# Gating products of reloaded activations placed behind the previous step's split, and 84 instead of 72 up products ahead

## The chip, the cores and the metric

The kernel runs on one core of one Trainium2 chip. The metric is the device time of one execution in microseconds (us); of several runs the median counts, and lower is better.

## The reference

Two blocks run one after the other on 256 latent and 256 context tokens of width 1024, in float32. The change lies in the first layer of the first block, in its feed-forward part over 16,384 experts:

```python
scores = einsum('bthpd,hpkd->bthpk', qr, subkeys)      # two halves of a query, 128 keys each
s1, i1 = top_k(scores[..., 0, :], 16); s2, i2 = top_k(scores[..., 1, :], 16)
top, pos = top_k(s1[..., :, None] + s2[..., None, :], 16)
eidx = (i1 * 128 + i2)[pos]; gate = softmax(top)
act = gelu(einsum('ted,td->te', u[eidx], h))
out = einsum('te,ted->td', gate * act, v[eidx])
```

Each token selects 8 x 16 experts; each expert is a row of `u` and a row of `v`.

## The kernel before

**Dense experts.** For three of the four token tiles (384 tokens) the kernel computes all 16,384 experts densely. They are cut into 128 chunks of 128. An *up* (`up0`, L1133) is one chunk's product with the 384 token columns: 24 matmuls of 384 columns in PSUM tile `pu`, a GELU on ScalarE into `act`, 128 x 384. Float32 is kept by splitting each operand into a high and a low half and multiplying three times (`mm3`, L292): a weight tile is loaded into `wr` (4 buffers), ScalarE casts the high half (`wh`, L286), VectorE subtracts it to get the low half (`wl`, L287). The loader `S0` has three `wh`/`wl` pairs, for ups and downs alike.

A *down* (`Down`, L849) multiplies the gated activations of one chunk with 128 rows of `v`: 18 matmuls of 512 columns, for three token tiles, accumulated in six PSUM banks over all 128 chunks. So no down can be finished before all gates are known.

**Gates.** `route0` (L1144) computes the queries and keys, the selection (`select`, VectorE), and then writes the gates of all 384 tokens as a dense table (`scatter`, L807, into `gd0` in DRAM), by one-hot matmuls of 128 columns. It is a generator: at each `yield x, y` the loop at L1205 adds `x` to a credit and traces that many ups beside the routing, and `y` to the steps of `own` (below). Ups that are computed before the gates exist are written to DRAM (`actd`, L1140) and read back later.

**The main loop** (L1250) runs over `j` = 0 to 129:

```python
again(j + 5)                       # reload of act j+5, ten act buffers
if j + 2 >= NA and done[0] < 128:
    up0()
if j < 128:
    weigh0(j)
...
if j >= LAG:                       # LAG = 2
    down0(j - LAG)
own_steps(0.5 if j + 2 < NA else 1.4)
```

`weigh0(i)` (L1226) loads the gates of eight chunks at once (`gsc`, 1.5 MB, two buffers), multiplies `act` by the gate on VectorE (L1232, called *the product* below), casts the high half `Wh` on ScalarE (L1236) and subtracts for the low half `Wl` on VectorE (L1237); `Wh` and `Wl` have four buffers. With `NA` = 72 the loop has two parts: a *reload part*, with downs alone, whose activations come back from DRAM, and a *late part*, in which each step has an up and a down.

**The fourth tile.** `own` (L1099) treats 128 tokens by gathering each one's experts: for each of 128 slots an indirect DMA from GpSimd's queue brings 8 KB per token (`uv`, 1 MB, four buffers), VectorE computes the dot product with `u` (L1118) and adds the weighted `v` (L1113). `own_steps(x)` places such steps behind the instruction in `mark[0]`, the last `Wl` of the loop (or the last one-hot in the scatter).

**What sets the order.** The engines' order is made by a scheduler at build time, by priorities and a model of durations; `tc.issue_after(ins)` adds an edge that keeps what is traced inside the block behind `ins` on its own engine. Each engine, and each DMA queue, then runs its list in order, and an instruction that waits holds up all that stands behind it. Loads and reloads are issued by SyncE (SP).

Of the kernel before, what the change touches and what calls it, by code (L numbers as in the profile page):

```python
# [29 lines left out]
OP = mybir.AluOpType  # L30
# [15 lines left out]
PK = 4  # L46
FA = 4
AH1 = 22
NA = 72
LAM_INIT = 0.8 - 0.6 * math.exp(0.0)  # L50


# [168 lines left out]
def body(ctx: ExitStack, tc: tile.TileContext, ap, stop=99):  # L221
    nc = tc.nc

    def pool(es, name, bufs=1, space=None, side=None):
        if space is None:
            return es.enter_context(tc.tile_pool(name=name, bufs=bufs, side=side, reuse_waits="tile"))
        return es.enter_context(tc.tile_pool(name=name, bufs=bufs, space=space))
# [35 lines left out]
    def pw(shape=(128, 512), name="pw"):  # L263
        return psP.tile(list(shape), F32, name=name, tag="ps")
# [32 lines left out]
    def prod_b(src, h, t0, n, sx=None, alloc=None, eng=None):  # L297
        wh, wl = (sx or S0).load(src, (128, DK, 128), eng=eng)
        ps = (alloc or pu)()[:, :n]
        c0 = t0 - h.base  # L300
        for k in range(DK):
            mm3(ps, wh[:, k], wl[:, k], h.hi[:, k, c0:c0 + n], h.lo[:, k, c0:c0 + n], k == 0, k == DK - 1)
        return ps
# [20 lines left out]
    def new_h(p, tag="h", base=0, n=512):  # L324
        h = K()
        h.base = base
        h.hi = p.tile([128, DK, n], F32R, name=tag + "hi")
        h.lo = p.tile([128, DK, n], F32R, name=tag + "lo")
        return h
# [29 lines left out]
    def sums(name):  # L359
        return sm.tile([128, 2], F32, name=name, tag=name, bufs=4)  # L360

    def sq_half(src, ss, nt):
        junk = sm.tile([128, 512], BF16, name="junk", tag="junk", bufs=1)
        nc.scalar.activation(junk, src, AF.Square, accum_out=ss[:, nt:nt + 1])
# [104 lines left out]
    def drain(it):  # L469
        for _ in it:  # L470
            pass

    def add_gated(t, nt, ps, g):
        ns = slice(nt * 512, nt * 512 + 512)
        tmp = sm.tile([128, 512], F32, name="agt", tag="agt", bufs=1)
        nc.vector.tensor_tensor(tmp, ps, g[:, ns], op=OP.mult)
        r = res(t)
        nc.vector.tensor_tensor(r[:, ns], r[:, ns], tmp, op=OP.add)
# [229 lines left out]
    def top16(rp, s, v, i, n):  # L708
        w = rp.tile([128, n], F32, name="mr", tag=f"mr{n}", bufs=2)
        nc.vector.max(v[:, 0:8], s)  # L710
        nc.vector.max_index(i[:, 0:8], v[:, 0:8], s)
        nc.vector.match_replace(w, v[:, 0:8], s, -3.0e38)
        nc.vector.max(v[:, 8:16], w)
        nc.vector.max_index(i[:, 8:16], v[:, 8:16], w)
# [88 lines left out]
    def turned(rp, T, tag="TT", tiles=range(2)):  # L803
        TT = rp.tile([128, 2, 4, 128], F32, name="TT", tag=tag, bufs=1)
        for t in tiles:
            ps = pw((128, 3, 128))
            for a in range(3):  # L807
                nc.tensor.transpose(ps[:, a], T[:, a, t], ident)
            nc.scalar.copy(TT[:, t, :3], ps)
            nc.vector.tensor_scalar(TT[:, t, 3], TT[:, t, 1], -1.0, None, op0=OP.mult)  # L810
        return TT

    mark = [None]
# [280 lines left out]
    gd0 = dp.tile([24, 128, 128, 16], F32, name="gd0")  # L1094
    actd = dp.tile([NA, 128, 384], F32, name="actd")
    eid = tp0.tile([128, 128], U32, name="eid")
# [31 lines left out]
    def act0():  # L1128
        return tp0.tile([128, 24, 16], F32, name="act", tag="act", bufs=10)
# [3 lines left out]
    def up0():  # L1133
        i = done[0]
        done[0] += 1
        pg = prod_b(ap["ut0"][i], hh, 0, 384)
        a = act0()
        nc.scalar.activation(a, pg.rearrange("p (a b) -> p a b", b=16), AF.Gelu)
        if i < NA:
            nc.scalar.dma_start(actd[i], a.rearrange("p a b -> p (a b)"))  # L1140
        else:
            late[i] = a

    def route0():  # L1144
        et, es = ExitStack(), ExitStack()
        hp = pool(et, "turned0")
        kp = pool(es, "keys0")
        rp = pool(es, "route0")
        tvs = [kp.tile([128, 2, 2, 8, 16], F32, name=f"tv{p}") for p in range(2)]
        tis = [kp.tile([128, 2, 2, 8, 16], U32, name=f"ti{p}") for p in range(2)]  # L1150
        Ts = [kp.tile([128, 3, 2, 128], F32, name=f"T{p}") for p in range(2)]

        def sel(p, half):
            return select(rp, tvs[p], tis[p], half, Ts[p], 2, (eid, egt) if p else None)
        s0 = sel(1, 0)
        for c in range(16):
            pq = prod_b(ap["wq0"][c], hh, 0, 512, eng=nc.gpsimd if c >= 4 else None)
            qT = kp.tile([128, 512], F32, name="qT", tag="qT", bufs=2)
            nc.scalar.copy(qT, pq)
            skey = kp.tile([128, 128], F32, name="skey", tag="skey", bufs=2)  # L1160
            nc.sync.dma_start(skey, ap["skey0"][:, c])
            ps = pw((128, 4, 128))
            for a in range(4):
                nc.tensor.matmul(ps[:, a], qT[:, a * 128:(a + 1) * 128], skey, start=True, stop=True)
            with tc.high_priority(offset=HP):
                for a in range(4):
                    p, t = divmod(a, 2)
                    top16(kp, ps[:, a], tvs[p][:, c // 8, t, c % 8], tis[p][:, c // 8, t, c % 8], 128)
            if c >= 8:
                next(s0, None)  # L1170
            yield (0.2 if c < 8 else 0.7), 0
        for _ in s0:
            yield 0.6, 0
        for _ in sel(1, 1):
            yield 0.6, 0
        for half in range(2):
            for _ in sel(0, half):
                yield 0.6, 0
        TX = turned(hp, Ts[1], "TTx", (0,))
        TC = turned(hp, Ts[0], "TTc")  # L1180
        es.close()
        yield 0, None
        op = pool(et, "scatter0")
        for k, TT in ((2, TX[:, 0]), (0, TC[:, 0]), (1, TC[:, 1])):
            for _ in scatter(op, TT, gd0[8 * k:8 * k + 8], 2):
                yield 0.42, 0.2
        et.close()

    def mods_ahead():
# [5 lines left out]
    def own_steps(x):  # L1195
        due[0] += x
        while due[0] >= 1:
            with tc.issue_after(mark[0].ins):
                next(mine, None)
            due[0] -= 1  # L1200
# [3 lines left out]
    for x, y in route0():  # L1204
# [7 lines left out]
        credit += x  # L1212
        while credit >= 1 and done[0] < NA:
            up0()
            credit -= 1
        own_steps(y)
    drain(fill)
    while done[0] < NA:
        up0()
# [4 lines left out]
    gates, acts, later = [None], {}, []  # L1224

    def weigh0(i):  # L1226
        if i % 8 == 0:
            gates[0] = gp0.tile([128, 24, 8, 16], F32, name="gsc", tag="gsc", bufs=2)
            nc.sync.dma_start(gates[0].rearrange("p a b c -> p a (b c)"),
                              gd0[:, :, i:i + 8].rearrange("a p i t -> p a (i t)"))  # L1230
        a = acts.pop(i) if i < NA else late.pop(i)
        nc.vector.tensor_tensor(a, a, gates[0][:, :, i % 8], op=OP.mult)  # L1232
        wh = ep.tile([128, 384], F32R, name="Wh", tag="Wh", bufs=4)
        wl = ep.tile([128, 384], F32R, name="Wl", tag="Wl", bufs=4)
        af = a.rearrange("p a b -> p (a b)")
        nc.scalar.copy(wh, af)  # L1236
        mark[0] = nc.vector.tensor_tensor(wl, af, wh, op=OP.subtract)  # L1237
        later.append((wh, wl))

    def again(i):  # L1240
        if i < NA:
            acts[i] = act0()
            nc.sync.dma_start(acts[i].rearrange("p a b -> p (a b)"), actd[i])
# [6 lines left out]
    for j in range(128 + LAG):  # L1250
        again(j + 5)
# [4 lines that stand above are left out]
        if j == 128 + LAG - 4:  # L1256
            drain(mine)
            for nt in range(2):
                add_gated(3, nt, yown[:, nt * 512:(nt + 1) * 512], g2x)
            css[3] = sums("nss")  # L1260
            for nt in range(2):
                sq_half(resx[:, 1, nt * 512:(nt + 1) * 512], css[3], nt)
            eO.close()
            h1 = new_h(pool(eM, "mixh1", 1, side="right"))
            c1 = ms[0, 1].coefs(1, 0, 1)
        if j >= LAG:
            down0(j - LAG)
        own_steps(0.5 if j + 2 < NA else 1.4)
    for t in (2, 3, 0, 1):
        with tc.high_priority(offset=2 * HP):  # L1270
            if t != 3:
# [433 lines left out]
```

## Time and profile before

| | us |
|---|---|
| median of three runs (lowest, highest) | 3767.36 (3761.19, 3768.62) |
| the profiled execution's own time | 3762.31 |
| its span | 3760.5 |
| TensorE busy in the span | 3518.7 (94%) |
| VectorE busy | 2509.4 (67%) |
| ScalarE busy | 1726.1 (46%) |
| GpSimd busy | 582.5 (15%) |

The span is what the profiler saw from the first to the last instruction; the own time is 1.8 us longer. A busy share is an average over stages with different limits, so the stages of the first layer's experts are told apart by time: keys and selection to about 735 us, scatter to 976 us, the turn to the main loop to 1004 us, the reload part to 1380 us, the late part to 1850 us. Granted clock 1.00 means that TensorE had its full 2.4 GHz all through a stretch.

### The profile page before, as it was taken

The page shows a single profiled execution, that of the slowest core. Times are in us where ns is not written, and L with a number is a line of the kernel's source. Part 1 is how long each engine was busy: PE and PEld are TensorE (multiplying, and loading weights), DVE is VectorE, ACT ScalarE, POOL GpSimd, SP SyncE. Part 2 cuts the span into 40 slices and gives each one's busy share as a digit, 9 for nine tenths or more (in the row PEclk, how much of TensorE's full clock was granted, in tenths as well). Part 3 has the DMA queues.
Part 4 walks back from the last instruction along what each step waited for, and adds up shares of the span by engine and source line. Part 5 has one row for each costly group of instructions (what it writes and reads, how often), then busy time and mean ns, then how long its engine had stood idle before and what let it go on. Part 6 is the DMA issues. An engine that isn't in the chain of part 4 may idle for free. (4 is left out here: it accounts for less than half of the span.)

```text
span 3760.5 us, 57378 instructions
## 1 busy us (share of the span) xinstructions
PE 3518.7 (94%) x21201; PEld 3044.2 (81%) x21201; DVE 2509.4 (67%) x5109; ACT 1726.1 (46%) x3173; POOL 582.5 (15%) x618
## 2 busy tenths in 40 slices
PE   7998998999887799999998899999999989898899
PEld 5776777799766679999886889988998868798798
DVE  5456698488655578787666799655555556656854
ACT  4323323466422234444443558444444445655464
POOL 0000110276200012222000327000000012001200
PEclk9999999999998999999999999999999989999999
DMA  6325447787977788888455456766665565654373
GB/s 232 125 97 183 143 160 278 286 286 276 308 262 247 250 285 322 321 325 323 162 163 181 165 171 242 249 209 214 216 212 197 188 216 185 207 180 150 125 261 105
DMA packets 293073, 818.89 MB, mean 218 GB/s; under 512 B 25303, under 2 KB 133496, under 8 KB 271096
## 3 DMA queue, kind: packets, MB, share of 16 engines
q1 hardware_dynamic: 263992, 666.83, 52.6%
q0 software_dynamic: 18432, 134.23, 9.7%
q10 hardware_dynamic: 10368, 14.16, 1.0%
q8 instruction: 168, 2.75, 0.3%
q14 instruction: 113, 0.93, 0.1%
HBM read 755.29 MB, written 59.83 MB: 217 GB/s over the span
## 5 line engine op out<-in xcount | busy, mean ns | idle before, releaser
L287 DVE TENSOR_TENSOR wl<-wr,wh 128x1024 fp32r<-128x1024 f32 x812 | 999.0, 1233 | 578.5 <-ACT wh L286 575.9
L286 ACT CAST wh<-wr 128x1024 fp32r<-128x1024 f32 x840 | 877.6, 1047 | 830.1 <-PE pu L294 497.2
L293 PE MATMUL pu<-hxhi,wh 128*128 128x256 f32 x1984 | 561.5, 283 | 6.3 <-ACT wh L286 4.1
L295 PE MATMUL pu<-hxhi,wl 128*128 128x256 f32 x1984 | 560.8, 283 | 0.8 <-DVE wl L287 0.8
L294 PE MATMUL pu<-hxlo,wh 128*128 128x256 f32 x1984 | 559.5, 282 | 0.2 <-DVE hxlo L404 0.2
L293 PE MATMUL pacc<-wh,Wh 128*128 128x512 f32 x1280 | 508.8, 398 | 0.0
L294 PE MATMUL pacc<-wl,Wh 128*128 128x512 f32 x1280 | 508.5, 397 | 0.0
L295 PE MATMUL pacc<-wh,Wl 128*128 128x512 f32 x1280 | 506.5, 396 | 0.0
L293 PE MATMUL pu<-hhhi,wh 128*128 128x384 f32 (+1 forms) x1152 | 403.3, 350 | 6.0 <-ACT wh L286 4.7
L295 PE MATMUL pu<-hhhi,wl 128*128 128x384 f32 (+1 forms) x1152 | 399.8, 347 | 6.7 <-DVE wl L287 6.4
L294 PE MATMUL pu<-hhlo,wh 128*128 128x384 f32 (+1 forms) x1152 | 398.6, 346 | 0.0
L293 PEld LDWEIGHTS pu<-hxhi,wh 128*128 128x128 f32 x1984 | 373.9, 189 | 15.2 <-ACT wh L286 4.9
L294 PEld LDWEIGHTS pu<-hxlo,wh 128*128 128x128 f32 x1984 | 374.2, 189 | 7.8 <-DVE hxlo L404 0.7
L295 PEld LDWEIGHTS pu<-hxhi,wl 128*128 128x128 f32 x1984 | 375.0, 189 | 1.2 <-DVE wl L287 1.0
L295 PEld LDWEIGHTS pacc<-wh,Wl 128*128 128x128 f32 x1280 | 242.9, 190 | 58.1
L1105 POOL DMA_INDIRECT uv<-in_uv_dram,eid x128 | 158.7, 1240 | 830.5 <-DVE yown L1113 682.5
L293 PEld LDWEIGHTS pacc<-wh,Wh 128*128 128x128 f32 x1280 | 243.6, 190 | 51.6
L294 PEld LDWEIGHTS pacc<-wl,Wh 128*128 128x128 f32 x1280 | 243.0, 190 | 51.0
L830 POOL TENSOR_SCALAR ohB<-iota,TT 128x128 f32<-128x128 f32 x320 | 241.0, 766 | 190.6 <-PE pw L836 99.2
L293 PEld LDWEIGHTS pu<-hhhi,wh 128*128 128x128 f32 x1152 | 217.8, 189 | 26.9 <-issue 7.8
L295 PEld LDWEIGHTS pu<-hhhi,wl 128*128 128x128 f32 x1152 | 218.0, 189 | 18.3 <-DVE wl L287 10.9
L827 DVE TENSOR_SCALAR ohA<-iota,TT 128x128 f32<-128x128 f32 x640 | 196.6, 359 | 50.0 <-PE pw L836 48.9
(418 smaller groups left out, 5952.9 us busy)
## 6 DMA issues: line engine op xcount, KB each, us to landing
wr<-in_ut_dram SPq DMA_DIRECT2D x256, 512.0 KB
wr<-in_v_dram SPq DMA_DIRECT2D x256, 512.0 KB
wr<-in_wmod_dram SPq DMA_DIRECT2D x176, 512.0 KB
wr<-in_wm_dram SPq DMA_DIRECT2D x128, 512.0 KB
wr<-in_winb_dram SPq DMA_DIRECT2D x48, 512.0 KB
gd<-stage SPq DMA_DIRECT2D x24, 1024.0 KB
gsc<-gd SPq DMA_DIRECT2D x16, 1536.0 KB
wr<-in_wq_dram SPq DMA_DIRECT2D x32, 512.0 KB
```

Of the source, the lines that this page charges most:

```text
L286: nc.scalar.copy(hi, r)
L287: (eng or nc.vector).tensor_tensor(lo, r, hi, op=OP.subtract)
L293: nc.tensor.matmul(ps, lh, rh, start=start, stop=False)
L294: nc.tensor.matmul(ps, lh, rl, start=False, stop=False)
L295: nc.tensor.matmul(ps, ll, rh, start=False, stop=stop)
L827: mark[0] = nc.vector.tensor_scalar(A, iota, TT[:, 0, tj], TT[:, 2, tj], op0=OP.is_equal, op1=OP.mult)
L830: nc.gpsimd.tensor_scalar(B, iota, TT[:, 1, tj], None, op0=OP.is_equal)
L1105: nc.gpsimd.indirect_dma_start(uv[s], None, ap["uv"], bass.IndirectOffsetOnAxis(ap=eid[:, s:s + 1], axis=0))
```

## The change

`NA` goes from 72 to 84: twelve ups move from the main loop to the time before it. Each of the 36 yields of the selection now gives credit for 0.9 instead of 0.6 ups. In the scatter, `own` steps come at 0.25 instead of 0.2 per yield; in the main loop at 0.45 instead of 0.5 in the reload part and 1.45 instead of 1.4 in the late part. The product gets an edge behind `mark[0]`, which is the `Wl` of the step before.

```diff
-NA = 72
+NA = 84
...
         for _ in s0:
-            yield 0.6, 0
+            yield 0.9, 0
         for _ in sel(1, 1):
-            yield 0.6, 0
+            yield 0.9, 0
         for half in range(2):
             for _ in sel(0, half):
-                yield 0.6, 0
+                yield 0.9, 0
...
             for _ in scatter(op, TT, gd0[8 * k:8 * k + 8], 2):
-                yield 0.42, 0.2
+                yield 0.42, 0.25
...
         a = acts.pop(i) if i < NA else late.pop(i)
-        nc.vector.tensor_tensor(a, a, gates[0][:, :, i % 8], op=OP.mult)
+        with tc.issue_after(mark[0].ins):
+            nc.vector.tensor_tensor(a, a, gates[0][:, :, i % 8], op=OP.mult)
...
-        own_steps(0.5 if j + 2 < NA else 1.4)
+        own_steps(0.45 if j + 2 < NA else 1.45)
```

In the built order, the reload part has 68 downs in a row before and 80 after. Ups ahead of the first down are 72 and 84: 6 beside the keys in both, 22 and 33 beside the selection, 44 and 45 from the scatter's start on.

**VectorE in the reload part, before.** `act` is the reloaded activation, `gsc` its gates, `Wl` the low half made of it, `wl` the low half of a tile of `v`; a higher number is a later step, and a new `act` takes the buffer of the tenth before it. `act_11329` takes that of `act_10985`:

```order
L1232 TENSOR_TENSOR act_11292<-act_11292,gsc_11261 128x384
L1237 TENSOR_TENSOR Wl_11158<-act_10985,Wh_11157 128x384
L1118 ISA uv_10983,dots_6171<-uv_10983,hn_2704 128x1024
L1118 ISA dots_6171 128x1
L287 TENSOR_TENSOR wl_11201<-wr_11198,wh_11200 128x1024
L1113 SCALAR_TENSOR_TENSOR yown_5941<-uv_10915,wts_6172,yown_5941 128x1024
L1232 TENSOR_TENSOR act_11329<-act_11329,gsc_11261 128x384
L1237 TENSOR_TENSOR Wl_11195<-act_11018,Wh_11194 128x384
L287 TENSOR_TENSOR wl_11232<-wr_11229,wh_11231 128x1024
```

The product of `act_11329` stands some nine steps ahead of its own `Wl`, and only one `wl` behind the `Wl` that gives its buffer free.

The same engine and place with the change; here `act_11512` takes the buffer of `act_11176`, whose `Wl` stands 40 rows ahead:

```order
L1233 TENSOR_TENSOR act_11444<-act_11444,gsc_11413 128x384
L287 TENSOR_TENSOR wl_11658<-wr_11655,wh_11657 128x1024
L1238 TENSOR_TENSOR Wl_11621<-act_11444,Wh_11620 128x384
L1233 TENSOR_TENSOR act_11481<-act_11481,gsc_11413 128x384
L1238 TENSOR_TENSOR Wl_11652<-act_11481,Wh_11651 128x384
L1233 TENSOR_TENSOR act_11512<-act_11512,gsc_11681 128x384
L287 TENSOR_TENSOR wl_11691<-wr_11688,wh_11690 128x1024
L1238 TENSOR_TENSOR Wl_11685<-act_11512,Wh_11684 128x384
```

Each product now stands right behind the `Wl` of the step before, nine `wl` rows behind the `Wl` that frees its buffer. Of every two steps, one has the product and its own `Wl` next to each other.

**SP's queue at a load of gates in the reload part, with the change.** `gsc_11681` is first read by the product of `act_11512` above:

```order
L278 DMA wr_11488<-in_v0_dram 128x1024
L1244 DMA act_11481<-actd_3043 128x384
L1244 DMA act_11512<-actd_3043 128x384
L1229 DMA gsc_11681<-gd0_3042 128x24x128
L278 DMA wr_11519<-in_v0_dram 128x1024
L1244 DMA act_11549<-actd_3043 128x384
L278 DMA wr_11556<-in_v0_dram 128x1024
```

The load stands between the loads of `v` for `wr_11488` and `wr_11519`; VectorE reaches the product behind `wl_11658`, which is made of `wr_11655`.

**SP's queue in the selection, before.** `in_wmod` are weights of the modulation, `in_ut0` those of an up:

```order
L278 DMA wr_4885<-in_wmod01_dram 128x1024
L278 DMA wr_4891<-in_ut0_dram 128x1024
L278 DMA wr_4936<-in_wmod01_dram 128x1024
L278 DMA wr_4955<-in_wmod01_dram 128x1024
L278 DMA wr_4961<-in_ut0_dram 128x1024
```

And with the change:

```order
L278 DMA wr_4825<-in_wmod01_dram 128x1024
L278 DMA wr_4831<-in_ut0_dram 128x1024
L278 DMA wr_4877<-in_wmod01_dram 128x1024
L278 DMA wr_4889<-in_ut0_dram 128x1024
L278 DMA wr_4936<-in_wmod01_dram 128x1024
```

A second modulation load often stood between two up loads; now they mostly alternate.

## Rows read from the trace of the kernel before

**Rows 1.** Busy time by stretch; after the engines: granted clock, DMA share, GB/s.

```profile
core 0: us, PE busy (x) PEld busy (x) DVE busy (x) ACT busy (x) POOL busy (x), PEclk, DMA share, GB/s
530.00:735.00 205.00, 184.67 (x1237) 148.47 (x1238) 139.76 (x536) 75.84 (x168) 29.25 (x34) 0.98 0.77 270
735.00:976.00 241.00, 239.25 (x1544) 231.46 (x1544) 200.54 (x507) 151.42 (x357) 154.00 (x181) 0.99 0.77 275
976.00:1004.00 28.00, 14.62 (x85) 14.30 (x83) 5.92 (x6) 6.59 (x11) 0.00 (x0) 0.82 1.04 345
1004.00:1380.00 376.00, 312.62 (x1222) 244.50 (x1223) 228.97 (x316) 113.24 (x210) 36.21 (x35) 0.91 0.78 261
1380.00:1800.00 420.00, 420.00 (x2113) 379.36 (x2112) 333.56 (x413) 177.03 (x342) 98.86 (x71) 1.00 0.88 323
```

**Rows 2.** Timeline: first down, two matmuls twelve apart, first up after the reloads.

```profile
1004.07 0.79 PE L293 MATMUL pw<-wh,Wh 128*128 128x512 f32 x1 [13.44 <-ACT Wh L1236]
...
1339.77 0.40 PE L293 MATMUL pacc<-wh,Wh 128*128 128x512 f32 x1
...
1342.57 0.40 PE L293 MATMUL pw<-wh,Wh 128*128 128x512 f32 x1
...
1380.55 0.34 PE L293 MATMUL pu<-hhhi,wh 128*128 128x384 f32 x1
```

**Rows 3.** Waits from 1004 to 1380 us: total us, times, longest.

```profile
PE pw L294 <- DVE wl L287: 63.2, 19, 6.8
...
DVE act L1232 <- DMA act<-actd: 139.7, 30, 10.3
...
SPq L1243 <- DVE Wl L1237: 153.2, 45, 7.1
...
ACT wh L286 <- DMA wr<-in_v_dram: 3.5, 1, 3.5
```

**Rows 4.** Timeline around 1203 us, one such wait.

```profile
1202.34 0.56 DVE L1232 TENSOR_TENSOR act<-act,gsc 128x384 f32<-128x384 f32 x1 [5.35 <-DMA act<-actd]
...
1204.42 1.22 DVE L287 TENSOR_TENSOR wl<-wr,wh 128x1024 fp32r<-128x1024 f32 x1
...
1205.70 0.79 PE L294 MATMUL pw<-wl,Wh 128*128 128x512 f32 x1 [3.26 <-DVE wl L287]
```

**Rows 5.** VectorE's groups by line from 1004 to 1380 us: busy us, mean ns, idle before.

```profile
L287 DVE TENSOR_TENSOR wl<-wr,wh 128x1024 fp32r<-128x1024 f32 x67 | 81.6, 1218 | 4.0 <-ACT wh L286 4.0
...
L1113 DVE SCALAR_TENSOR_TENSOR yown<-uv,wts,yown 128x1024 f32<-128x1024 f32 x36 | 46.0, 1277 | 0.0
L1118 DVE CUSTOM_DVE_ANT_0 uv<-uv,hn 128x1024 f32<-128x1024 f32 x36 | 43.8, 1217 | 0.0
L1237 DVE TENSOR_TENSOR Wl<-act,Wh 128x384 fp32r<-128x384 f32 x71 | 39.1, 551 | 3.4 <-ACT Wh L1236 3.4
L1232 DVE TENSOR_TENSOR act<-act,gsc 128x384 f32<-128x384 f32 x70 | 38.3, 554 | 139.7 <-DMA act<-actd 139.7
```

**Rows 6.** DMA, 1004 to 1380 us: gathers' queue (packets, MB, share); issues with sizes.

```profile
q0 software_dynamic: 4919, 35.84, 26.4%
...
wr<-in_v_dram SPq DMA_DIRECT2D x65, 512.0 KB
gsc<-gd SPq DMA_DIRECT2D x9, 1536.0 KB
act<-actd SPq DMA_DIRECT2D x62, 192.0 KB
...
uv<-in_uv_dram,eid POOLq DMA_INDIRECT x35, 8.2
```

**Rows 7.** Timeline of the turn: reloads issued behind the gates' load, first product.

```profile
990.77 15.11 SPq L1243 DMA_DIRECT2D act<-actd  x12
...
1002.87 1.03 DVE L1232 TENSOR_TENSOR act<-act,gsc 128x384 f32<-128x384 f32 x2 [10.08 <-DMA act<-actd]
```

**Rows 8.** ScalarE's and SP's waits from 545 to 735 us (selection).

```profile
ACT wh L286 <- DMA wr<-in_ut_dram: 50.8, 18, 9.5
...
SPq L278 <- PE pacc L433: 92.6, 31, 6.8
```

**Rows 9.** VectorE's waits from 735 to 976 us (scatter).

```profile
DVE ohA L827 <- PE pw L836: 35.5, 33, 3.4
```

## The prediction

> **What bounds the kernel now.** I read the busy times by stretch first. TensorE is the bound nearly everywhere in the first layer's experts: 99% busy in the scatter, 100% in the late part [rows 1]. The exceptions are the selection (184.67 of 205 us), the turn, and the reload part: from 1004 to 1380 us it is busy 312.62 of 376 us, at a mean granted clock of 0.91, while the late part runs at 1.00 [rows 1].
>
> The timeline gives the reload part's length: the first down starts at 1004.07 us, the first up after it at 1380.55 us [rows 2], 376.5 us for the 68 downs of the order, 5.54 us each. Undisturbed, twelve matmuls of 512 columns start in 1342.57 - 1339.77 = 2.80 us [rows 2], so the 18 of a down take 4.20 us and 68 take 285.6 us. The stage loses 90.9 us.
>
> The waits say to what. TensorE waited 63.2 us in 19 waits for VectorE's `wl` [rows 3]; the other 27.7 us are matmuls at the lower clock after such waits. VectorE itself stood 139.7 us in 30 waits before the product, until a reload landed [rows 3]. The tiles of `v` are not what is late: ScalarE waited for one once, 3.5 us [rows 3]. One case shows the chain: the product waits 5.35 us, the `wl` queued behind it comes at 1204.42 us, and TensorE, short of it, has stood 3.26 us [rows 4]. SP waited 153.2 us before reloads for a `Wl` [rows 3]. With the order this is a closed loop: a reload is issued only when the `Wl` ten steps older frees its buffer, and VectorE meets that reload's product one step later, so it stands through the whole landing.
>
> **The change, part by part.** The sum is made against the profiled execution, 3762.3 us by its own time, 5.1 us below the median of 3767.4.
>
> *The edge.* The product now stands nine `wl` behind the `Wl` that frees its buffer, nine steps of at least 4.20 us, 38 us. The landing at the worst moment, behind the first gates, took from 990.77 to 1002.87 us, 12.1 us [rows 7]. So the wait for reloads goes. What is late next?
>
> TensorE's own pace is 4.20 us a step. VectorE's step: product 0.554, `Wl` 0.551, `wl` 1.218, and 0.45 `own` steps of 1.277 + 1.217 us = 1.12, together 3.45 us [rows 5]. Added is a turn over ScalarE where a product and its own `Wl` are neighbours: from the product's start at 1002.87 us to the matmul that its high half released at 1004.07 us [rows 7, 2] are 1.20 us, 0.65 of them past the product; in one step of two that is 0.33 us. 3.8 us a step lies under 4.20, with 10% to spare.
>
> DMA's step: 512 KB of `v`, 192 KB of reload, an eighth of 1536 KB of gates, and 0.45 of a gather of 35.84 MB / 35 [rows 6], in all 0.524 + 0.197 + 0.197 + 0.461 = 1.379 MB. The stage moved 261 GB/s at a busy share of 0.78 [rows 1], so 335 GB/s at a share of one, or 4.12 us a step. That is just under TensorE's 4.20. The late part held 323 GB/s with TensorE 100% busy [rows 1], which would be 4.27 us.
>
> So a step lies between 4.20 and today's 5.54 us, nearest to the late part's rate. With two resources both nearly full and the gates arriving in lumps of 1.5 MB, I take 4.4 us (313 GB/s, a share of 0.93), and 4.2 to 4.9 for the range. Eighty downs take 352 us instead of 376.5 for 68: **-24.5 us**.
>
> The Trainium skill, DMA: Bandwidth & Descriptors, section Specifications, puts the HBM limit of one core at about 358 GB/s. By that a step's bytes would need only 3.85 us, DMA would never bind, eighty downs would take 336 us and the sum would be 16 us lower. No stretch here shows that rate; the highest is 345 GB/s in the turn [rows 1], at a share of 1.04, so the trace's own ceiling is used.
>
> *Twelve ups leave the late part.* There 2113 matmuls at 42 a step are 50.3 steps in 420 us [rows 1], 8.35 us a step, of which the up is 4.15. Twelve steps of up and down go: 12 x 8.35 = **-100.2 us** (their downs are among the eighty). The ups come back earlier: 12 x 4.15 = **+49.8 us**, eleven of them beside the selection.
>
> *Idle filled in the selection.* TensorE idles 20.3 us there [rows 1]. ScalarE waits 50.8 us for up weights, and SP 92.6 us for modulation matmuls that hold load buffers [rows 8]. With loads alternating, each modulation load has an up's 4.15 us beside it. Bounds: nothing is filled, or all 20.3. I take half, **-10 us**, since the selection's chains on VectorE stay.
>
> *The turn.* TensorE stood 13.44 us before the first down [rows 2], until gates and reloads had landed [rows 7]. The queues' order there is unchanged, so nothing; at best one up more in the tail covers 4.2 us.
>
> *Scatter.* Five `own` steps more, 5 x 2.5 = 12.5 us of VectorE in 241 us. VectorE waits 35.5 us there for TensorE [rows 9], which covers them: nothing. If that cover were gone, up to 12 us.
>
> *Late part.* Own steps at 1.45 are 0.12 us more of VectorE in 8.35, which is busy 333.56 of 420 us [rows 1]: nothing. But 24 + 36.9 + 63.8 steps are traced by `j` = 126, against 132.6 before, so the last four run together beside the last downs, ahead of the last product on VectorE. Four are 10 us beside four downs of 16.8 us: I take **+2 us**, bounds 0 and 10.
>
> Sum: -24.5 - 100.2 + 49.8 - 10 + 2 = -82.9 us, 3679.4 by the profiled run's scale, **3684 us** by the median's (2.2% faster).
>
> **The rivals.** *DMA binds.* If the lumps of gates and the gathers delay `v` so that a step takes 5.0 us (276 GB/s, between the 261 of now and the 323 of the late part), eighty take 400 us: 3732 us. For it: the turn's 28 us ran at a share of 1.04 [rows 1]. Against: the late part moves more per us without a wait of TensorE.
>
> *VectorE binds.* If most steps pay the 0.65 us turn and behind it another for ScalarE's `wh`, a step is 3.45 + 1.3 = 4.75 us, 380 us in all: 3712 us. Against: TensorE has two steps of `wl` in store.
>
> *The edge does nothing.* If the reload wait only reappears elsewhere and a step stays at 5.54 us, eighty take 443 us, +91: 3775 us, just slower than now. Against: the lead grows from one step to nine.
>
> *The gates' load becomes the wait, and the kernel is slower.* Products no longer run ahead, so a `gsc` buffer is freed later, and SP waits for it with `v` loads behind. If each of ten loads exposed its 12.1 us [rows 7] on eighty steps of 4.20 us, the part takes 457 us: 3789 us. It decides if the load is issued less than about three steps ahead of its first product. Against: in the order about eight loads of `v` are consumed between, some 34 us.
>
> **How the numbers follow.** A measurement of this kernel can tell about 0.2% from no change, 3759.8 to 3774.9 us. Chances: forecast 0.72, DMA binds 0.11, VectorE binds 0.09, edge does nothing 0.04, gates' load 0.04. The first three are all faster, 0.92; the edge's case ends at the upper bound of no change, so its 0.04 is split: same 0.02, slower 0.06. The range's low end is 4.22 us a step (-14), the selection's idle all filled (-10), the turn's 4 and the tail's 2: 3654. The high end is 4.9 us a step (+40), nothing filled (+10) and 6 us of tail: 3740, which takes in both binding rivals. What lies outside has about 0.15.
>
> **What would show it.** In the new profile VectorE's wait before L1233 for `act<-actd` should fall from 139.7 to under 15 us; the reload part should hold 80 downs in 340 to 370 us at a granted clock of 0.97 or more and a DMA share above 0.88; TensorE's wait for `wl` should be under 15 us. Late steps should stay at 8.35 us, the selection grow by some 36 us. The prediction is wrong if waits of ScalarE for `v` or for gates take the reloads' place, or if the selection grows by the full 46 us.

## The result and the profile after

The changed kernel took 3670.23 us (median of four runs, 3667.03 to 3670.86), the kernel before beside it 3766.99 (3761.19 to 3768.62): a ratio of 0.9744, with a 95% interval from 0.9727 to 0.9761. It is 2.6% faster. The profiled execution took 3670.57 us, its span is 3668.8 us, 91.7 us shorter than before.

Busy time by stretch (TensorE, its weight loads, VectorE, ScalarE, GpSimd; then granted clock, DMA share, GB/s), the answer to [rows 1]; the third row is the turn, the fourth the reload part, the fifth the late part:

```profile
530.00:735.00 205.00, 191.40 (x1206) 163.11 (x1204) 129.14 (x478) 70.04 (x140) 6.95 (x6) 0.97 0.75 248
736.00:1020.00 284.00, 279.33 (x1831) 262.93 (x1830) 238.58 (x595) 176.14 (x414) 180.67 (x212) 0.99 0.82 294
1022.00:1050.00 28.00, 17.07 (x99) 16.75 (x97) 6.62 (x6) 7.21 (x10) 0.70 (x1) 0.90 1.00 323
1050.00:1388.00 338.00, 337.29 (x1438) 270.29 (x1439) 260.39 (x356) 136.65 (x236) 36.41 (x36) 0.99 0.94 329
1388.00:1740.00 352.00, 352.00 (x1770) 317.87 (x1769) 286.97 (x356) 149.32 (x293) 89.35 (x63) 1.00 0.89 327
```

In the reload part TensorE is busy 337.29 of 338 us where it was 312.62 of 376, at a granted clock of 0.99 for 0.91, and DMA moves 329 GB/s for 261. The timeline gives the stage's borders, as [rows 2, 7] did (start, duration, instruction; in brackets the idle time before and what ended it):

```profile
1036.15 0.42 SPq L1229 DMA_DIRECT2D gsc<-gd  x1
1039.51 11.70 SPq L1244 DMA_DIRECT2D act<-actd  x10
...
1049.51 0.56 DVE L1233 TENSOR_TENSOR act<-act,gsc 128x384 f32<-128x384 f32 x1 [8.27 <-DMA act<-actd]
...
1050.71 0.79 PE L293 MATMUL pw<-wh,Wh 128*128 128x512 f32 x1 [11.64 <-ACT Wh L1237]
...
1388.49 0.34 PE L293 MATMUL pu<-hhhi,wh 128*128 128x384 f32 x1
...
1771.57 2.05 PE L382 MATMUL pw<-dg,resx 128*128 128x128 f32 x16 [0.38 <-DVE dg L377]
```

Eighty downs take from 1050.71 to 1388.49 us, 337.8 us or 4.22 us each, where a step took 5.54. The last row is the first matmul of the work behind the experts, so the late part is 383.1 us. Before, the same matmul stood here in the timeline, 481.0 us behind the first later up:

```profile
1861.60 2.05 PE L382 MATMUL pw<-dg,resx 128*128 128x128 f32 x16 [0.60 <-DVE dg L377]
```

The waits from 1050 to 1388 us (total us, times, longest) answer to [rows 3]:

```profile
DVE Wl L1238 <- ACT Wh L1237: 57.4, 46, 2.0
...
DVE wl L287 <- ACT wh L286: 20.2, 36, 1.2
...
PE pw L293 <- ACT Wh L1237: 11.6, 1, 11.6
DVE act L1233 <- DMA act<-actd: 8.3, 1, 8.3
...
ACT wh L286 <- DMA wr<-in_v_dram: 4.8, 3, 2.4
```

VectorE's wait for reloads is one of 8.3 us, the first, where there were 139.7 us in 30. TensorE's only wait is that for the first down; the 63.2 us for `wl` are gone. ScalarE's wait for `v` is 4.8 us where it was 3.5 [rows 3], so nothing has taken the reloads' place. VectorE now waits 57.4 us for `Wh`, its own `Wl` standing right behind the product, and TensorE does not wait for it. Of the signs that the prediction named, the wait under 15 us, the clock of 0.97 or more, the DMA share above 0.88 and TensorE's missing wait for `wl` are there; the length, named as 340 to 370 us, is 2 us under its lower end.

### The profile page after: what moved, and what is told of

Same layout as the page of the kernel before. It is cut to its first block, busy times and chain, and to the rows that moved or that the text cites. A ratio compares the mean times of both kernels' runs of the same rounds, so it can differ in the third digit from the quotient of the medians.

```text
span 3668.8 us, 57384 instructions
## 1 busy us (share of the span) xinstructions
PE 3495.9 (95%) x21201; PEld 3028.7 (83%) x21201; DVE 2514.7 (69%) x5109; ACT 1735.7 (47%) x3173; POOL 583.3 (16%) x618
## 5 line engine op out<-in xcount | busy, mean ns | idle before, releaser
L286 ACT CAST wh<-wr 128x1024 fp32r<-128x1024 f32 x840 | 880.6, 1050 | 909.0 <-PE pu L294 484.3
L295 PEld LDWEIGHTS pacc<-wh,Wl 128*128 128x128 f32 x1280 | 239.9, 187 | 57.4
```

The source lines that it names most:

```text
L286: nc.scalar.copy(hi, r)
L295: nc.tensor.matmul(ps, ll, rh, start=False, stop=stop)
```

## The experiments

The table splits each profiled span (us). *Selection* runs from the end of the keys' matmuls to the first one-hot product, *scatter* to the last one-hot, *turn* (with the last ups ahead) to the first down, *reload* to the first later up, with the number of downs, *late* to the first matmul behind the experts. Of what is left out, the time up to the keys' end is 549.7 before, 554.9 after and 552.5 to 559.3 elsewhere, and what follows the experts 1895 to 1905 in all. The borders are those of TensorE's matmuls. In the kernel before, the first one-hot product stands here, so its selection ends at 688.6 us and not at about 735, as the stretches of [rows 1, 8] took it:

```profile
688.58 1.16 PE L836 MATMUL pw<-ohA,ohB 128*128 128x128 f32 x8
```

| kernel | selection | scatter | turn | reload (downs) | late | span |
|---|---|---|---|---|---|---|
| before | 138.9 | 286.8 | 28.7 | 376.5 (68) | 481.0 | 3760.5 |
| changed | 181.3 | 283.5 | 31.0 | 337.8 (80) | 383.1 | 3668.8 |
| e1_edge_alone | 143.4 | 284.8 | 29.0 | 287.9 (68) | 481.0 | 3682.5 |
| e2_no_edge | 181.3 | 283.8 | 29.9 | 441.1 (80) | 383.1 | 3768.9 |
| e3_before_6_buffers | 133.1 | 284.8 | 29.2 | 386.1 (68) | 481.0 | 3771.7 |
| e4_own_070 | 183.1 | 282.6 | 30.1 | 353.5 (80) | 380.7 | 3684.8 |
| e5_after_6_buffers | 172.1 | 282.0 | 29.8 | 337.8 (80) | 382.9 | 3661.0 |
| e6_credit_060 | 141.6 | 289.6 | 68.5 | 338.8 (80) | 383.3 | 3673.7 |
| e7_early_reloads | 178.0 | 283.3 | 22.0 | 336.6 (80) | 383.1 | 3654.4 |
| e8_after_again | 179.7 | 281.1 | 30.0 | 338.1 (80) | 382.9 | 3671.3 |
| e9_7_buffers_early | 174.1 | 283.2 | 20.5 | 336.7 (80) | 383.2 | 3654.2 |
| e10_3_buffers | 172.8 | 282.6 | 30.1 | 346.6 (80) | 386.8 | 3673.5 |

The theory was the closed loop of the prediction: a reload goes out when a `Wl` frees its buffer, and VectorE met its product one step later, with `wl` queued behind. Rivals were that the twelve ups carry the gain, that the number of `act` buffers sets it, and that VectorE or DMA binds next. The first four runs share 19 runs of the kernel before (median 3771.31 us), e5 to e7 nine (3770.16), e8 to e10 nine (3772.73).

**The edge alone.** The kernel before, with the edge and nothing else:

```diff
-        nc.vector.tensor_tensor(a, a, gates[0][:, :, i % 8], op=OP.mult)
+        with tc.issue_after(mark[0].ins):
+            nc.vector.tensor_tensor(a, a, gates[0][:, :, i % 8], op=OP.mult)
```

> The kernel before with nothing but the edge that keeps each product behind the Wl of the step before. Theory (the loop of buffer release, reload and product is the whole loss): the 68 downs of the reload part fall from 376.5 us to 68 x 4.22 = 287 us, VectorE's wait for reloads from 139.7 us to under 15, the time to about 3677 us (3670 to 3690). Rival (the ups that were moved earlier carry much of the gain): no more than half of it comes from the edge, 3720 us or above.

It took 3682.32 us, a ratio of 0.9758 (0.9738 to 0.9778). Its reload part, by stretch and by waits (from 1013 to 1302 us):

```profile
1014.00:1301.00 287.00, 287.00 (x1221) 229.97 (x1222) 228.80 (x311) 119.69 (x206) 34.22 (x34) 0.99 0.96 336
```

```profile
PE pw L293 <- ACT Wh L1237: 13.8, 1, 13.8
...
DVE act L1233 <- DMA act<-actd: 10.4, 1, 10.4
```

The 68 downs take 4.23 us each, TensorE is never idle among them, and of the waits for reloads only the first is left. Of the other stages in the table none moved by more than 5 us. So the edge alone brings nearly the whole gain: 2.4 of 2.6%.

**The change without the edge.** Eighty-four ups and all the rates, the product as before (the diff of the first run, reversed, on the changed kernel).

> The changed kernel without the edge: 84 ups ahead and all the new rates stay. Theory: the reload part stays at about 5.5 us a step, now for 80 downs, 443 us instead of 338; the time is about 3775 us, no better than the kernel before or a little worse. Rival (moving ups beside the selection pays by itself): 3700 to 3740 us.

It took 3774.00 us, a ratio of 1.0005 (0.9995 to 1.0015), no gain. The waits from 1050 to 1490 us:

```profile
DVE act L1232 <- DMA act<-actd: 174.4, 44, 10.5
...
PE pw L294 <- DVE wl L287: 69.4, 28, 7.1
```

The old waits are back, and a down takes 441.1 / 80 = 5.51 us. Twelve more ups ahead are worth nothing here: the twelve downs that lose their ups are moved into a stage whose step is 5.5 us.

**Fewer buffers, without the edge.** In the built order of the kernel before some 1.5 `wl` rows stand between the `Wl` that frees a buffer and the reload's product; with six buffers 1.2. With the edge it is 9.3 to 9.5 with ten buffers.

```diff
-        return tp0.tile([128, 24, 16], F32, name="act", tag="act", bufs=10)
+        return tp0.tile([128, 24, 16], F32, name="act", tag="act", bufs=6)
```

> The kernel before, without the edge, with 6 instead of 10 buffers for the activations. Theory: what counts is the distance on VectorE between the Wl that frees a buffer and the product of the reload that takes it, and that is 1.2 wl rows here against 1.5 before, so the step stays near 5.5 us and the time within 15 us of 3767. Rival (too few buffers, or too shallow a prefetch, is what starves the stage): four buffers less make the step clearly longer, at 6.5 us or more, and the time 3830 us or above.

It took 3779.55 us, a ratio of 1.0019 (1.0008 to 1.0030), and the step is 386.1 / 68 = 5.68 us. VectorE's waits for reloads, from 1007 to 1392 us, against 139.7 us in 30 [rows 3]:

```profile
DVE act L1232 <- DMA act<-actd: 144.4, 30, 10.4
```

Four buffers of ten hardly matter, since without the edge the scheduler puts each product right behind the `Wl` that frees its buffer, however many there are.

**Six and three buffers, with the edge.** The same line in the changed kernel, with 6 (e5) and with 3 (e10); the distance is then 5.3 and 2.4 rows.

> The changed kernel with 6 instead of 10 buffers for the activations. The product now stands 5 wl rows behind the Wl that frees its buffer instead of 9. Theory (lead against landing): 5 steps of 4.22 us are 21 us, more than the 8 to 12 us of a landing, so the reload part stays at 338 us and the time within 8 us of 3670. Rival (depth of the prefetch matters in itself): waits for reloads come back, the step is 4.5 us or more, the time 3695 us or above.

> The changed kernel with 3 buffers for the activations: the product stands 2.4 wl rows behind the Wl that frees its buffer, some 10 us at 4.22 us a step, against landings of 8 to 12 us. Theory (lead against landing): the waits for reloads come back in part, VectorE waits 20 to 100 us for them, a step takes 4.4 to 5.0 us, the reload part 350 to 400 us. Rival (the place of the product in the queue alone cures the stage, whatever the lead): 4.22 us, 338 us.

Six take 3662.32 us, 0.9712 (0.9688 to 0.9736), with the same reload part to a tenth, 337.8 us, in which no product waits for a reload and TensorE waits for the first down alone; three take 3670.27, 0.9728 (0.9703 to 0.9752). With three the waits come back in part (from 1050 to 1390 us):

```profile
DVE act L1233 <- DMA act<-actd: 55.6, 20, 7.3
...
PE pw L294 <- DVE wl L287: 5.0, 5, 1.4
```

The step is 346.6 / 80 = 4.33 us. VectorE's waits came back as forecast, but the stage did not: 4.33 us and 346.6 us lie under the 4.4 to 5.0 and 350 to 400 us expected, nearer to the rival's 4.22 and 338. With the edge, then, a distance of 9.3 or 5.3 rows costs TensorE nothing and one of 2.4 about 0.1 us a step; without it, 1.5 rows cost 1.3. The distance, and not the number of buffers by itself, decides whether VectorE waits: six buffers with the edge do better than ten without. How much of the fall from 1.3 to 0.1 us is the longer distance, and how much the product's new place close to its own `Wl`, these runs do not separate. Here 55.6 us of VectorE's waits cost TensorE 5.0 us; a likely reason, not tested, is that none is longer than 7.3 us, against 10.3 before, and that TensorE has tiles of `wl` in store.

Six buffers gave something that no theory had foreseen: the selection is 9 us shorter in the trace. In the totals this is not resolved, since the interval of the ratio overlaps that of the changed kernel. From 650 to 700 us the stretch reads, in the changed kernel and then with six buffers:

```profile
650.00:700.00 50.00, 45.09 (x279) 38.95 (x278) 12.92 (x22) 13.04 (x19) 4.03 (x4) 0.93 0.86 302
```

```profile
650.00:700.00 50.00, 50.00 (x331) 43.09 (x331) 14.15 (x23) 14.82 (x22) 0.00 (x0) 1.00 0.83 264
```

The waits from 640 to 705 us, again of the changed kernel and then with six:

```profile
POOL uv L1105 <- DMA actd<-act: 118.2, 2, 117.9
ACT wh L286 <- DMA wr<-in_ut_dram: 43.6, 10, 9.0
```

```profile
ACT wh L286 <- DMA wr<-in_ut_dram: 26.1, 9, 4.5
```

The first gather of the fourth tile starts at 653.3 us in the changed kernel, after 117.9 us of waiting that the profile puts down to the writing out of an `act`, and at 535.7 with six buffers. In the first case its 1 MB gathers run beside the up weights: DMA moves 302 GB/s, ScalarE waits longer for weights and TensorE idles 4.9 of 50 us. All three kernels with the change and at most seven buffers start the gathers at 536 to 538 us and have a selection of 172 to 174 us, against 178 to 183 for the five with ten buffers and the same credits. Without the other changes it is alike: with six buffers the kernel before starts its gathers at 537.7 us instead of 646.1, and its selection is 133.1 us instead of 138.9. The orders of TensorE, VectorE and ScalarE are the same with ten and six there. That the buffers' place in memory sets what the gather waits for is argued from this, not shown; in the kernel before, the profile puts the same wait, 113.3 us, down to an instruction of ScalarE.

**More of the fourth tile in the reload part.**

```diff
-        own_steps(0.45 if j + 2 < NA else 1.45)
+        own_steps(0.7 if j + 2 < NA else 1.05)
```

> The changed kernel with 0.7 instead of 0.45 own steps per step in the reload part and 1.05 instead of 1.45 in the late part: the gathers move into the reload part, 1.635 instead of 1.379 MB a step. If DMA's ceiling is the 335 GB/s that the kernel before gave, a step takes 4.88 us, the reload part 390 us, the time 3722 us, and VectorE waits for gathers. If VectorE's order binds first, 3.45 + 0.25 x 2.5 + 0.33 = 4.4 us, 352 us, 3684 us. If both still have room, the step stays at 4.22 us and the time at 3670.

It took 3688.03 us, 0.9778 (0.9757 to 0.9798). Its reload part, by stretch and by waits:

```profile
1052.00:1405.00 353.00, 344.80 (x1440) 269.16 (x1440) 299.96 (x409) 142.77 (x271) 75.69 (x56) 1.00 1.00 365
```

```profile
ACT Wh L1237 <- DVE act L1233: 73.6, 48, 2.3
ACT wh L286 <- DMA wr<-in_v_dram: 41.3, 16, 4.9
DVE wl L287 <- ACT wh L286: 33.3, 12, 4.3
...
PE pw L293 <- ACT Wh L1237: 18.2, 15, 10.8
```

A step is 353.5 / 80 = 4.42 us, where the prediction's sum for VectorE gives 2.32 + 0.7 x 2.49 + 0.33 = 4.40. Yet VectorE, busy 299.96 of 353 us, is not alone: DMA stands at a share of 1.00, and ScalarE waits 41.3 us for `v`. Here both have reached TensorE's pace; which of them sets the 4.42 this run does not tell. At 0.45 neither does.

**The ups in the tail instead of beside the selection.** The three credits of the selection back at 0.6, `NA` still 84, so that the ups left over run in one piece ahead of the loop:

```diff
-            yield 0.9, 0
+            yield 0.6, 0
```

> The changed kernel with 0.6 instead of 0.9 ups per yield of the selection, 84 ups ahead as before it; the eleven ups then stand between the scatter and the first down. Theory (the selection's idle time was filled little, 3.6 us by the two traces): 3674 us, +4 (0 to +7). Rival, the forecast's term: +10, 3680 us. Second rival: the ups serve the turn better than the selection, and the time falls below 3667.

It took 3675.45 us, 0.9751 (0.9731 to 0.9770). Selection, scatter and turn together are 499.7 us, against 495.8 and 490.8 in the two profiled runs of the changed kernel (below). Beside the selection is the better place by 4 to 9 us in these traces; the intervals of the totals overlap. Part of what the selection would have given comes back in the turn: with the longer tail ahead of it, TensorE's wait before the first down is 3.4 us.

**Reloads ahead of the last ups.** The largest idle time that is left is the 11.64 us before the first down: the reloads are issued behind the gates' load. Here the first five reloads, with the definition of `again`, are traced ahead of the last ups:

```diff
+    for i in range(5):
+        again(i)
     while done[0] < NA:
         up0()
...
-    for i in range(5):
-        again(i)
```

> The changed kernel with the first five reloads traced ahead of the last ups, so that SP issues them before the first gates. Theory (the turn's 11.6 us of idle TensorE end with reloads that queue behind two loads of gates): the first product comes when the first gates have landed, the idle time falls to 2 to 4 us, the time to about 3661 us. Rival (the gates themselves, or the tiles of v behind them, are last): the idle time stays, 3670 us.

It took 3656.22 us, 0.9695 (0.9675 to 0.9716). TensorE's wait before the first down, which was 11.6 us:

```profile
PE pw L293 <- ACT Wh L1246: 2.6, 1, 2.6
```

The turn is 22.0 us for 31.0, the 9 us that the wait gave up.

**The changed kernel again, and both gains together.** The changed kernel unedited (e8), and beside it on the same chip one with seven buffers, three reloads ahead of the last ups and two behind (e9).

> The changed kernel once more, for a comparison on one chip with the two others of this group and with its own first runs: 3670 us, within 6.

> The changed kernel with 7 buffers for the activations and the first three reloads traced ahead of the last ups. Theory (two separate gains add): the first gathers start near 536 us instead of 653 and leave the selection's loads alone, 172 instead of 181 us; the turn's idle time falls from 11.6 to 2 to 4 us; the reload part stays at 338 us with the product 6 wl rows behind the Wl that frees its buffer. In all about 3650 us. Rival (the shorter selection of the kernel with 6 buffers was chance): 3660 us, the early reloads alone.

The changed kernel took 3670.38 us, 0.9730 (0.9712 to 0.9748), the other 3655.95, 0.9690 (0.9670 to 0.9709); each of its runs (at most 3656.69) lies below each of e8's (at least 3664.53). Its selection is 174.1 and its turn 20.5 us, as the two gains say. But the total lies between the 3650 us of the theory and the 3660 of the rival, and is that of e7, whose selection is 178.0: whether the second gain adds to the first is not resolved by these runs. Both beat the two kernels of the case, by 3.1% against before.

## Why the prediction was right

Forecast were 3684 us in a range from 3654 to 3740, and faster with 0.92. The median is 3670, 14 us below, within the range. Term by term, in spans of the profiled runs:

- *The edge, -24.5 forecast, -38.7 measured.* The mechanism held: the product no longer meets a reload that has not landed, the clock rose from 0.91 to 0.99, nothing else became the bound. The loop was drawn too strictly: VectorE does not stand through the landing at each reload, for 30 waits [rows 3] stand against 62 reloads in the stage [rows 6]. Mis-sized was "I take 4.4 us" for a step. It measured 4.22, at the low end of my 4.2 to 4.9, and 80 x 0.18 are 14 us. I had put DMA's ceiling at 335 GB/s from a stage that was not full, and allowed for lumps. The stage ran at 329 GB/s and a share of 0.94 with TensorE at its own 4.20, and the run with more gathers showed 365.
- *The late part and its tail, -98.2 forecast, -97.9 measured.* 1770 matmuls in 352 us are 42.1 steps of 8.35 us, as before.
- *The ups ahead and the idle filled, +39.8 forecast, +41.4 measured* for selection, scatter and turn together. That these agree so well is luck, for the parts came out otherwise. The selection grew by 42.4 us for eleven ups of 4.15, 45.7 us, so only 3 us were filled where I took 10, and it came near the 46 at which I had called the prediction wrong; scatter and turn together came out 5.1 us lower than the one up that I had put there. The 20.3 us of idle TensorE that I halved were read from a stretch, 530 to 735 us, that holds 20 us of the keys and 46 of the scatter. The selection proper, before and with the change, idles 14.9 and 10.4 us:

```profile
549.70:688.60 138.90, 124.02 (x831) 99.81 (x829) 101.64 (x394) 49.47 (x112) 7.20 (x8) 0.99 0.79 277
```

```profile
554.90:736.20 181.30, 170.95 (x1105) 146.06 (x1104) 114.69 (x404) 65.62 (x134) 5.80 (x7) 0.98 0.80 263
```

In the same two stretches ScalarE's wait for up weights doubled:

```profile
ACT wh L286 <- DMA wr<-in_ut_dram: 42.6, 14, 9.5
```

```profile
ACT wh L286 <- DMA wr<-in_ut_dram: 91.3, 28, 9.0
```

- *Scatter, nothing forecast for the five own steps.* It measured 3.3 us less with as much of the ups in it (970 and 967 matmuls of 384 columns), and the repeat of the changed kernel 5.7 less; the cover held. With the edge alone, which leaves the scatter as it was, it is 2.0 us less too, so I do not lay the rest to the change.
- *The turn, nothing forecast.* It grew by 2.3 us with one more up of 4.15 in it (86 such matmuls before, 110 after; an up has 24); TensorE's wait before the first down fell from 13.44 [rows 2] to 11.64 us.
- *Not in the sum:* the time up to the keys' end is 5.2 us longer. It ranges from 549.7 to 559.3 us over all twelve profiled runs, and is 556.7 with the edge alone, which touches nothing ahead of the main loop; so I do not lay it to the change.

Together -91.7 us (with -1.7 behind the experts), against -82.9, so the sum was off by 8.8 us: the 14 of the edge less some 5 of the rest. The medians differ by 96.8, since the profiled run of before lay 4.7 us under its median and that of the changed kernel 0.3 over. The 5.1 us that I added to go from the one scale to the other did not show in the changed kernel, and that the median misses the forecast by the same 14 us as the edge's term is chance.

What the sum did not say is how the parts hang together. Ahead of the experts' end, from the selection on, the spans are 1311.9 us before, 1226.1 with the edge alone, 1319.2 with all but the edge, 1216.7 with both. The edge is worth 86 us on 68 downs and 102 on 80; the ups cost 7 us without it and give 9 with it (14 in the repeat). These are single traces; in the totals the ups' part is not clear of noise, 1.0005 (0.9995 to 1.0015) without the edge, and with it two ratios whose intervals overlap, 0.9758 for the edge alone and 0.9744. The move itself is even at best: a late step of 8.35 us becomes a down of 4.22 and an up of 4.15, 8.37 us, and at 5.51 us a down it costs 1.3 us each. What it wins with the edge is idle time filled.

Of the rivals, "the edge does nothing" fell with the first two runs. "DMA binds" and "VectorE binds" did not come at 0.45 own steps, where TensorE waits for nothing after the first down, and came near only at 0.7. "The gates' load" fell too: no product waited for `gsc` in the stage, as the row of VectorE's waits shows, whose only load is `act`. The figure that I set aside as unseen, the 358 GB/s for a core of the Trainium skill, DMA: Bandwidth & Descriptors, section Specifications, would have given an estimate of 3668 us; the trace agrees with what follows from it, that DMA does not bind at 4.20 us a step.

## What to carry to other kernels

Where an in-order engine consumes a reload, count the rows between the instruction that frees the buffer and the one that consumes what is loaded into it, and compare the time they take with the landing: the number of buffers hardly matters if the consumer is queued right behind the release (ten gave a step of 5.54 us, six 5.68). The waiting engine needs not be the bound to cost time: look at what stands behind the waiting instruction and who is fed from it. And move work into a stage only after its step has been mended, since the same move was worth nothing at 5.5 us a step, and then count what it fills.

## What the runs showed of the hardware

With more gathers in the reload part DMA held 365 GB/s for 353 us at a busy share of 1.00, where the 28 us of the turn moved 323 at 1.00 (345 at 1.04 before). So a full share is not one rate, and a rate scaled up from another stage, the 335 GB/s of the prediction, is no ceiling; that the mix of transfers makes the difference is likely, but no run separates it. The Trainium skill, HBM Reference, section Specifications (TRN2), says that a core that streams alone measures well above its 358 GB/s, about 425; this run agrees as far as it goes, 2% above 358, and no stage here came near 425.

Changing only how many buffers `act` has, from ten to six, moved the start of the first gather by 118 us and the selection by 9 us in the changed kernel, by 108 and 6 in the kernel before; in the changed kernel the order on the three busiest engines is the same up to there.
